# A third block's output projection split by branch, and the first weight steps of two seven-product stages reordered

## The chip, the cores and the metric

One core of one Trainium2 chip runs the whole program. The metric is device time in microseconds, the median of three runs; beside it stands one execution that was taken with the hardware profiler, and all rows below come from that one. The engines are PE (matmul), DVE (vector), ACT (activation), POOL (GpSimd) and SP, which here only issues DMAs. Each works through its own instructions strictly in the order in which the program emits them, so an instruction that waits holds up everything behind it on its engine.

## What is computed

Three transformer-like blocks run one after the other on an input of 1024 tokens by 1024 channels, in float32.

1. Block 1: retention and a spatial gate, an output projection, then a feed-forward layer of width 2816 with a short convolution.
2. Block 2: a convolution branch and a neighbourhood attention branch, then an output projection.
3. Block 3, which the change is mostly about:

```python
merged = concatenate([rms_norm(sb_out, sb_norm_g), rms_norm(swa_out, swa_norm_g)])
h = layer_norm(ALPHA * h + merged @ w_out)
h = layer_norm(ALPHA * h + (silu(gate) * up) @ w_down)     # gate, up = split(h @ w_gate_up)
```

`sb_out` is a stick-breaking attention over all earlier tokens (8 heads of 64), `swa_out` a softmax attention over a local window of 128 tokens (8 heads of 64). Rows 0 to 511 of `w_out` belong to the first, rows 512 to 1023 to the second, here called the SB part and the local part.

## The kernel before

**Data.** Activations lie transposed, channels on the 128 partitions, in two halves of 512 tokens. Every float32 matmul operand is split into a high part and a rest (`hhi`/`hlo` for activations, `whi`/`wlo` for weights), and a product takes three matmuls of 128x512: hi by hi, lo by hi, hi by lo. A weight tile is 128x1024; `w_load` (L369) takes its raw form from a DMA, rounds it on ACT (`whi`) and subtracts on POOL (`wlo`). Four such tiles exist at a time: `w_take` hands them out, `w_retire` loads the next ones.

**Order.** The order of emission is written by hand. A main generator issues big matmuls in sixes and yields a cost; `Driver` (L191) then runs background generators, up to 1.5 times that cost, each of which yields a cost and a delay. `force` emits all that is left of one generator on the spot. `Belt` (L235) is such a generator: it carries attention items, each in three steps (`sb1` scores, sigmoids, running product; `sb2` transposes; `sb3` times values), with a lag between the steps; `until(n)` emits items until n are done.

**Block 3's middle.** In a loop over four head pairs p (from L2258) the query and key projections (`qk`) run as main work, and the 24 items of the pair before run beside them. After the loop the 24 items of the last pair are left. From L2319 on the program emits the items one after the other up to the 80th of 96 with `fsb.until`, with no main work beside them, and between them two of the four `gen_mix` calls (L2289), which read the local branch back from DRAM (`yd`), scale it, transpose it (`yt`) and split it into the matmul operand. Then `out_abba` (L582) runs the whole output projection, 8 tiles of output channels by 2 halves by 8 chunks of input channels, with tiles `op` in PSUM: half 0 first, where the last 16 items run beside it, then half 1. It reloads four weight tiles for half 1, so it takes 12. After each half, `done` (L2376) starts the layer norm `gen_ln` (L651) of that half in the background: sums, mean, subtract, squares, row of factors, then 8 chunks, each scaled and split for the feed-forward's first matmuls (`fq`), which need them.

**Feed-forward.** `first_quad` (L548) runs the first matmuls, `fq`, over the two halves, and calls `hook(n)` (L1346) eight times, every 24 matmuls. In the hooks and behind them the six weight steps of the first seven-product group are emitted (`s_steps`, L1203): `s0` splits a quarter (`shi` on ACT, `slo` on POOL), `s1` makes two sums on POOL in place (`raw`), `s2` splits both, `s3` splits a whole tile (`whi`, `wlo`), `s4` makes two more sums, `s5` splits a second whole tile, which the next group's first product needs. `strassen` (L1256) then runs groups of seven products of 12 matmuls; in each it emits the six steps of the group after it. In a group `e1` is a copy of the first bank on ACT, `v1` adds the second bank to it on DVE, and the fourth product writes into that second bank, so it cannot start ahead of `v1`. Block 1 calls it with `lead=3` (a third pair of tiles runs as plain matmuls first), block 3 with `lead=2`.

Of the kernel before, what the change touches and what calls it, by code (L numbers as in the profile page):

```python
# [39 lines left out]
def _weights(a):  # L40
# [52 lines left out]
    t += abba(wa("w_out_3", 0, 1024))  # L93
# [5 lines left out]
S_TILES = ((38, 38), (178, 180))  # L99
# [199 lines left out]
class Kernel:  # L299
# [956 lines left out]
    def strassen(self, put, left, later, rest, tail):  # L1256
# [21 lines left out]
        for n in range(n_all):  # L1278
# [5 lines left out]
            if n + 1 < n_all:  # L1284
                steps = self.s_steps(n + 1, nxt)
                steps[0]()
                steps[1]()
            else:
                tail(0)
# [4 lines left out]
            if n == 0:  # L1294
                steps[2]()
                yield from prod(b2, cur["S24"], 0, T[2], True)
# [5 lines left out]
            if n == 0:  # L1302
                rest()
# [28 lines left out]
    def ffn(self, evac, put, later, add_last, done, by_half, alpha=None, lead=2):  # L1332
# [5 lines left out]
        with ExitStack() as ctx:  # L1338
# [7 lines left out]
            def hook(n):  # L1346
# [3 lines left out]
                elif n in (1, 2, 3):  # L1350
# [55 lines left out]
            if lead == 3:  # L1406
                ws = self.w_take(2)
                for f in steps:
                    f()
                self.s_dma(1)  # L1410
                for half in (1, 0):
                    for w in range(2):
                        ps = self.bank("fq")
                        yield from self.gemm_a(ps, ws[w], half)
                        put(2, w, half, ps, None)
                    if half:
# [553 lines left out]
    def block3(self):  # L1970
# [8 lines left out]
        roomy = []  # L1979

        def tmp(name):
            return self.h(name) if roomy else tp.tile([128, HF], F32, tag="t", name=name)
# [61 lines left out]
        def y_put(p, n, e, branch, ssq, write):  # L2044

            own = branch == 0 and p == 3
            if own:
                yc = Y[n][:, 384 + 64 * e:448 + 64 * e]
            else:
                if e == 0:  # L2050
                    YS[branch, p, n] = self.small(128, "ys")
                yc = YS[branch, p, n][:, 64 * e:64 * e + 64]
# [3 lines left out]
            if e == 1 and not own:  # L2056
# [200 lines left out]
        self.w_retire(2)  # L2257
        for p in range(4):  # L2258
            ws = self.w_take(2)
            for half in range(2):  # L2260
                for w in range(2):
# [25 lines left out]
        H2 = self.new_h()  # L2287

        def gen_mix(half, b):  # L2289

            n0 = 4 * half
            if not b:
                r = self.small(4, "r1")
                token_rms(r, ssb[:, n0:n0 + 4, :])
                ys = Y[n0:n0 + 4]
            else:
                r = rsw[:, n0:n0 + 4]
                ys = [self.h("yr") for _ in range(4)]
                for n in range(4):
                    nc.sync.dma_start(out=ys[n], in_=self.yd[n0 + n][:, 512:1024])  # L2300
                yield 0.0, 0.0
            for n in range(4):
                self.ts(ys[n], ys[n], r[:, n:n + 1])
            yield 0.0, 8470.0
            for c in range(4):
                ps = self.bank("yt")
# [160 lines left out]
```

## Time and profile before

| what | us |
|---|---|
| median of three runs | 3127.25 (3125.31 to 3131.94) |
| the profiled execution, device time | 3131.53 |
| its span, first to last instruction | 3129.7 |
| PE busy in the span | 2941.2 (94%) |
| DVE, POOL, ACT busy | 1803.3, 1432.9, 1284.8 |
| mean granted clock of PE | 0.964 of full |

The page's chain of work that ended last is made of PE lines for the largest part, and PE is busy in 94% of the span. So a saving must come from the few stretches in which PE stands still or runs at the lower clock. In the forty slices of the page these show as a digit below 9 in the rows PE and PEclk.

### The profile page before, as it was taken

Reading aid. Unit: us, or ns where it says so; the run is one execution under the profiler, and the core shown is the slowest. Engines: PE = TensorE matmul, PEld = TensorE weight load, DVE = VectorE, ACT = ScalarE, POOL = GpSimd, SP = SyncE. Lnnn points to the kernel's source line nnn. Section 1 sums busy time; section 2 is a strip of 40 time slices with the busy share of each in tenths; the row PEclk is TensorE's granted clock in tenths of the full one; section 3 lists DMA queues with packets and bytes.
Section 4 is the critical chain, followed back from the end, with each engine's and each line's share of the span. In section 5 each row is a group of like instructions: output and inputs, shape, how many; then the busy total and the mean of one; then the engine's idle time right before and its main releaser. Section 6 shows DMA issues by size and latency. Waiting matters only on the chain. (4 is left out here: it accounts for less than half of the span.)

```text
span 3129.7 us, 41397 instructions
## 1 busy us (share of the span) xinstructions
PE 2941.2 (94%) x15188; PEld 2499.6 (80%) x15188; DVE 1803.3 (58%) x3522; ACT 1284.8 (41%) x2493; POOL 1432.9 (46%) x1008
## 2 busy tenths in 40 slices
PE   8999998999999999889998989989899899999997
PEld 6898776888878877868897778977678688888886
DVE  6444246666665569966645665577667522224556
ACT  4232224444432153556673356654444422222223
POOL 4313434777743365862214342144333477774330
PEclk9999999999999999999998989999889999999998
DMA  4101241222252312131113232110222222225321
GB/s 159 33 23 51 72 134 41 81 81 81 81 188 82 108 49 80 40 109 50 44 39 118 84 121 64 42 32 27 68 68 98 84 81 81 86 79 179 108 81 54
DMA packets 114876, 248.96 MB, mean 80 GB/s; under 512 B 19696, under 2 KB 31600, under 8 KB 114672
## 3 DMA queue, kind: packets, MB, share of 16 engines
q1 hardware_dynamic: 114384, 246.01, 24.0%
q8 instruction: 120, 1.97, 0.3%
q14 instruction: 84, 0.69, 0.1%
q10 hardware_dynamic: 288, 0.30, 0.0%
HBM read 192.52 MB, written 53.74 MB: 79 GB/s over the span
## 5 line engine op out<-in xcount | busy, mean ns | idle before, releaser
L332 POOL TENSOR_TENSOR wlo<-raw,whi 128x1024 fp32r<-128x1024 f32 x240 | 582.2, 2436 | 862.0 <-ACT whi L326 846.5
L326 ACT ACTIVATE whi<-raw 128x1024 fp32r<-128x1024 f32 x240 | 248.3, 1053 | 537.0 <-PE dn L347 283.2
L332 DVE TENSOR_TENSOR X<-dn,X 128x512 f32<-128x512 f32 (+1 forms) x312 | 209.9, 676 | 161.7 <-PE dn L347 159.5
L347 PE MATMUL dn<-ghi,whi 128*128 128x512 f32 (+1 forms) x736 | 281.1, 382 | 0.6 <-DVE X L332 0.6
L347 PE MATMUL dn<-glo,whi 128*128 128x512 f32 (+1 forms) x736 | 280.2, 381 | 0.0
L347 PE MATMUL dn<-ghi,wlo 128*128 128x512 f32 (+1 forms) x736 | 280.2, 381 | 0.0
L332 POOL TENSOR_TENSOR raw<-raw 128x512 f32<-128x512 f32 x156 | 203.0, 1302 | 12.1
L332 POOL TENSOR_TENSOR slo<-raw,shi 128x512 fp32r<-128x512 f32 x117 | 150.7, 1302 | 106.2 <-ACT shi L326 104.9
L347 PE MATMUL p<-thi,shi 128*128 128x512 f32 x468 | 185.1, 395 | 13.9 <-DVE u L1105 9.8
L332 DVE TENSOR_TENSOR v<-p,e 128x512 f32<-128x512 f32 x78 | 53.8, 690 | 243.8 <-ACT e L326 194.3
L347 PE MATMUL p<-tlo,shi 128*128 128x512 f32 x468 | 183.9, 393 | 0.0
L347 PE MATMUL p<-hhi,wlo 128*128 128x512 f32 x468 | 182.2, 389 | 1.7 <-POOL wlo L332 1.7
L347 PE MATMUL p<-thi,slo 128*128 128x512 f32 x468 | 183.7, 393 | 0.0
L347 PE MATMUL p<-hhi,whi 128*128 128x512 f32 x468 | 182.1, 389 | 0.0
L347 PE MATMUL p<-hlo,whi 128*128 128x512 f32 x468 | 182.1, 389 | 0.0
L329 DVE SCALAR_TENSOR_TENSOR t<-u,vec,t 128x512 f32<-128x512 f32 x176 | 132.9, 755 | 79.5 <-ACT t L326 74.2
L347 PE MATMUL qk<-hhi,whi 128*128 128x512 f32 x384 | 162.2, 422 | 7.8 <-ACT hhi L326 7.2
L332 POOL TENSOR_TENSOR beta<-beta,f 128x511 f32<-128x511 f32 (+3 forms) x96 | 91.2, 956 | 154.0 <-DVE beta L336 137.8
L347 PEld LDWEIGHTS dn<-ghi,whi 128*128 128x128 f32 x736 | 139.2, 189 | 27.6 <-DVE X L332 1.3
L347 PEld LDWEIGHTS dn<-ghi,wlo 128*128 128x128 f32 x736 | 139.1, 189 | 26.4
L347 PEld LDWEIGHTS dn<-glo,whi 128*128 128x128 f32 x736 | 139.2, 189 | 26.0
L347 PE MATMUL op<-hhi,wlo 128*128 128x512 f32 x384 | 153.2, 399 | 4.0 <-POOL wlo L332 4.0
(400 smaller groups left out, 8150.7 us busy)
## 6 DMA issues: line engine op xcount, KB each, us to landing
raw<-in_wall SPq DMA_DIRECT2D x240, 512.0 KB, 3.8
gd<-g SPq DMA_DIRECT2D x88, 256.0 KB, 2.2
gx<-gd SPq DMA_DIRECT2D x88, 256.0 KB, 5.2
x2d<-X SPq DMA_DIRECT2D x64, 256.0 KB, 2.0
X<-x2d SPq DMA_DIRECT2D x64, 256.0 KB, 5.3
x<-in_xT SPq DMA_DIRECT2D x16, 256.0 KB, 6.0
X<-in_xT SPq DMA_DIRECT2D x16, 256.0 KB, 4.6
T<-in_rpbx SPq DMA_DIRECT2D x8, 448.0 KB, 3.6
```

The source lines that it names most:

```text
L326: self.nc.scalar.activation(out=out, in_=in_, func=func, bias=bias, scale=scale, **kw)
L329: self.nc.vector.scalar_tensor_tensor(out=out, in0=in0, scalar=s, in1=in1, op0=op0, op1=op1)
L332: (eng or self.nc.vector).tensor_tensor(out=out, in0=in0, in1=in1, op=op)
L347: self.nc.tensor.matmul(out=out, lhsT=lhsT, rhs=rhs, start=start, stop=stop, skip_group_check=more)
```

## The change

The third block's weight tiles of `w_out` are laid out by branch: four tiles for the local rows, then four for the SB rows, each with two output tiles side by side; 8 tiles are taken instead of 12. `out_abba` and the waits from L2319 on are gone. `gen_mix` moves ahead of the pair loop; the local mix of half 0 is put to the background in the last pair's second half, that of half 1 right after the loop. The local part of the projection (8 calls of `out_part`) then runs as main work with the last 24 items beside it, and writes ALPHA times the input plus its product back to X. The SB part follows, half 0 and half 1 with four calls each, and adds to X. So each X tile gets two additions from PSUM instead of one. The last head pair's attention output now goes to DRAM and back like that of the other pairs, and the items' temporaries keep their ten buffers to the end. In the feed-forward the steps `s0` to `s2` move: in block 1 from hooks 1, 2, 3 to hooks 3, 5, 7, with `s5` behind the first plain matmuls' evacuation; in the first group of both blocks, the next group's `s0` to `s2` move behind `e1` and `v1`.

```diff
--- before.py
+++ after.py
@@ -90,13 +90,15 @@
     q, k = wa("w_in_3", 0, 512), wa("w_in_3", 512, 1024)
     for p in range(4):
         t += [q[p], k[p]]
-    t += abba(wa("w_out_3", 0, 1024))
+    o = wa("w_out_3", 0, 1024)
+    for c in (slice(512, 1024), slice(0, 512)):
+        t += [np.concatenate([o[2 * i][:, c], o[2 * i + 1][:, c]], axis=1) for i in range(4)]
     t += ffn("w_gate_up_3", "w_down_3")
     return np.stack(t)
 
 
 
-S_TILES = ((38, 38), (178, 180))
+S_TILES = ((38, 38), (174, 176))
 
 _VEC = [
     ("mix_norm_g", 8), ("ret_norm_g", 4), ("ffn_norm_g", 8), ("conv_b", 44), ("final_norm_g", 8),
@@ -1283,8 +1285,9 @@
                 self.s_dma(n + 2)
             if n + 1 < n_all:
                 steps = self.s_steps(n + 1, nxt)
-                steps[0]()
-                steps[1]()
+                if n > 0:
+                    steps[0]()
+                    steps[1]()
             else:
                 tail(0)
             if n > 0:
@@ -1292,7 +1295,6 @@
                 steps[2]()
             yield from prod(b1, cur["A1"], 0, B11, True)
             if n == 0:
-                steps[2]()
                 yield from prod(b2, cur["S24"], 0, T[2], True)
             if n + 1 == n_all:
                 tail(1)
@@ -1300,6 +1302,8 @@
             self.act(e1, b1, AF.Copy)
             self.tt(v1, b2, e1, ALU.add)
             if n == 0:
+                for f in steps[0:3]:
+                    f()
                 rest()
             steps[3]()
             for f in left[0]:
@@ -1347,7 +1351,7 @@
 
                 if n == 0 and lead == 3:
                     self.s_dma(0)
-                elif n in (1, 2, 3):
+                elif n in ((1, 2, 3) if lead == 2 else (3, 5, 7)):
                     steps.pop(0)()
                 elif n in (4, 6):
                     next(gt)
@@ -1405,14 +1409,16 @@
             left = ([], [], [])
             if lead == 3:
                 ws = self.w_take(2)
-                for f in steps:
-                    f()
+                steps.pop(0)()
+                steps.pop(0)()
                 self.s_dma(1)
                 for half in (1, 0):
                     for w in range(2):
                         ps = self.bank("fq")
                         yield from self.gemm_a(ps, ws[w], half)
                         put(2, w, half, ps, None)
+                        if steps:
+                            steps.pop(0)()
                     if half:
                         next(gt)
                         next(gt)
@@ -1976,10 +1982,9 @@
         po2 = ctx.enter_context(tc.tile_pool(name="b3p", bufs=2, space=PSUM))
         ctx1 = ExitStack()
         kp = ctx1.enter_context(tc.tile_pool(name="b3k", bufs=4))
-        roomy = []
 
         def tmp(name):
-            return self.h(name) if roomy else tp.tile([128, HF], F32, tag="t", name=name)
+            return tp.tile([128, HF], F32, tag="t", name=name)
 
         identb = pp.tile([128, 128], mybir.dt.bfloat16, tag="ib", bufs=1, name="identb")
         sbmb = pp.tile([128, 128], mybir.dt.bfloat16, tag="mb", bufs=1, name="sbmb")
@@ -2043,17 +2048,13 @@
 
         def y_put(p, n, e, branch, ssq, write):
 
-            own = branch == 0 and p == 3
-            if own:
-                yc = Y[n][:, 384 + 64 * e:448 + 64 * e]
-            else:
-                if e == 0:
-                    YS[branch, p, n] = self.small(128, "ys")
-                yc = YS[branch, p, n][:, 64 * e:64 * e + 64]
+            if e == 0:
+                YS[branch, p, n] = self.small(128, "ys")
+            yc = YS[branch, p, n][:, 64 * e:64 * e + 64]
             write(yc)
             sq = self.small(64, "ysq")
             self.act(sq, yc, AF.Square, accum=ssq[:, n, 2 * p + e:2 * p + e + 1])
-            if e == 1 and not own:
+            if e == 1:
                 nc.sync.dma_start(out=self.yd[n][:, 512 * branch + 128 * p:512 * branch + 128 * p + 128],
                                   in_=YS.pop((branch, p, n)))
 
@@ -2255,9 +2256,39 @@
         fsw.put(*[sw_unit(p, n) for p in range(4) for n in range(4, 8)])
         yield from values(ws, 1, range(3, 8))
         self.w_retire(2)
+        H2 = self.new_h()
+
+        def gen_mix(half, b):
+
+            n0 = 4 * half
+            ys = [self.h("yr") for _ in range(4)]
+            for n in range(4):
+                nc.sync.dma_start(out=ys[n], in_=self.yd[n0 + n][:, 512 * b:512 * b + 512])
+            r = rsw[:, n0:n0 + 4]
+            if not b:
+                r = self.small(4, "r1")
+                token_rms(r, ssb[:, n0:n0 + 4, :])
+            yield 0.0, 4000.0
+            for n in range(4):
+                self.ts(ys[n], ys[n], r[:, n:n + 1])
+            yield 0.0, 2500.0
+            for c in range(4):
+                ps = self.bank("yt")
+                for n in range(4):
+                    nc.tensor.transpose(ps[:, 128 * n:128 * n + 128], ys[n][:, 128 * c:128 * c + 128], self.ident)
+                hi, lo = self.h("hhi", F32R), self.h("hlo", F32R)
+                H2[0][c + 4 * b][half], H2[1][c + 4 * b][half] = hi, lo
+                g = self.v("swa_norm_g_3" if b else "sb_norm_g_3", c)
+                self.act(hi, ps, AF.Identity, scale=g)
+                self.stt(lo, ps, g, hi, ALU.mult, ALU.subtract)
+                yield 450.0, 200.0
+
+        sws, sbs = [None, None], [None, None]
         for p in range(4):
             ws = self.w_take(2)
             for half in range(2):
+                if p == 3 and half == 1:
+                    sws[0] = drv.add(gen_mix(0, 1))
                 for w in range(2):
                     ps = self.bank("qk")
                     yield from self.gemm_a(ps, ws[w], half)
@@ -2284,54 +2315,6 @@
                 fsb.put(*[u[i, e][0] for i in (3, 0, 2, 1) for e in range(2)])
                 fsb.put(*[u[i, e][x] for i in (7, 6, 5, 4) for x in range(2) for e in range(2)])
 
-        H2 = self.new_h()
-
-        def gen_mix(half, b):
...
-                ys = Y[n0:n0 + 4]
-            else:
...
-                for n in range(4):
-                    nc.sync.dma_start(out=ys[n], in_=self.yd[n0 + n][:, 512:1024])
-                yield 0.0, 0.0
-            for n in range(4):
-                self.ts(ys[n], ys[n], r[:, n:n + 1])
-            yield 0.0, 8470.0
...
-        roomy.append(True)
-        fsb.lag = 6
-        sws = [gen_mix(0, 1), gen_mix(1, 1)]
-        next(sws[0])
-        next(sws[1])
-        fsb.until(70)
-        next(sws[0])
-        fsb.until(72)
-        Y = [self.h("yr") for _ in range(8)]
-        for n in range(8):
-            nc.sync.dma_start(out=Y[n][:, 0:384], in_=self.yd[n][:, 0:384])
-        drv.force(sws[0])
-        next(sws[1])
-        fsb.until(76)
-        drv.force(sws[1])
-        fsb.until(80)
-        sbs = [drv.add(gen_mix(0, 0)), None]
-        self.H = H2
         X = [[None, None] for _ in range(8)]
         self.X = X
         acc, seen = [None, None], [[], []]
@@ -2351,11 +2334,6 @@
             elif n > 2:
                 self.tt(acc[half], acc[half], X[j][half][:, sl], ALU.add)
 
-        def o_evac(j, half, ps):
-            x = X[j][half]
-            self.stt(x, x, ALPHA, ps, ALU.mult, ALU.add)
-            acc_x(j, half)
-
         def ln1_sink(half):
             def sink(j, x, b):
                 hi, lo = self.h("hhi", F32R), self.h("hlo", F32R)
@@ -2379,15 +2357,56 @@
             acc[half] = None
             seen[half] = []
 
-        def middle():
-
-            fsb.finish()
-            ctx1.close()
-            ctx.close()
-            sbs[1] = drv.add(gen_mix(1, 0))
-
-        yield from self.out_abba(o_load, o_evac, done, (4, 5, 6, 7, 0, 1, 2, 3), lambda half: None,
-                                 lambda half: drv.force(sbs[half]), middle)
+
+        def out_part(w, t, half, b):
+            pss = [self.bank("op") for _ in range(2)]
+            whi, wlo = w
+            for k in range(4):
+                hi, lo = H2[0][4 * b + k][half], H2[1][4 * b + k][half]
+                for i, ps in enumerate(pss):
+                    c = slice(512 * i + 128 * k, 512 * i + 128 * k + 128)
+                    self.mm(ps, whi[:, c], hi, k == 0, False)
+                    self.mm(ps, whi[:, c], lo, False, False)
+                    self.mm(ps, wlo[:, c], hi, False, k == 3)
+                yield 6 * 216.0
+            for i, ps in enumerate(pss):
+                x = X[2 * t + i][half]
+                if b:
+                    self.stt(x, x, ALPHA, ps, ALU.mult, ALU.add)
+                else:
+                    self.tt(x, ps, x, ALU.add)
+                    acc_x(2 * t + i, half)
+
+        sws[1] = drv.add(gen_mix(1, 1))
+        drv.force(sws[0])
+        for t in (0, 2):
+            ws = self.w_take(2)
+            for half in range(2):
+                for j in range(2 * t, 2 * t + 4):
+                    o_load(j, half)
+            for half in range(2):
+                if half and not t:
+                    drv.force(sws[1])
+                if half and t:
+                    fsb.until(80)
+                    sbs[0] = drv.add(gen_mix(0, 0))
+                for i in range(2):
+                    yield from out_part(ws[i], t + i, half, 1)
+                    if half:
+                        self.w_retire(1)
+        ws = self.w_take(4)
+        for half in range(2):
+            drv.force(sbs[half])
+            for t in range(4):
+                if half == 0 and t == 2:
+                    fsb.finish()
+                    ctx1.close()
+                    ctx.close()
+                    sbs[1] = drv.add(gen_mix(1, 0))
+                yield from out_part(ws[t], t, half, 0)
+                if half:
+                    self.w_retire(1)
+            done(half)
         self.H, self.hs, self.rs = H3, new_hs, None
 
         A = {}
```

## Rows read from the trace of the kernel before

**Rows 1.** Busy time by stretch: stretch, length, then each engine's us, PEclk, DMA share, GB/s

```profile
2170.60:2239.00 68.40, 62.17 (x388) 51.35 (x388) 47.99 (x105) 33.93 (x96) 30.23 (x30) 0.97 0.09 24
2236.40:2288.20 51.80, 38.14 (x188) 33.31 (x189) 35.42 (x76) 24.11 (x67) 19.65 (x17) 0.62 0.36 117
2288.20:2337.50 49.30, 47.56 (x294) 40.92 (x294) 31.95 (x73) 20.58 (x50) 18.89 (x14) 0.98 0.23 72
2337.50:2407.00 69.50, 69.50 (x332) 58.17 (x331) 46.51 (x70) 25.76 (x38) 17.80 (x8) 1.00 0.29 95
2500.00:2600.00 100.00, 100.00 (x441) 82.14 (x440) 24.88 (x37) 28.65 (x42) 70.61 (x47) 1.00 0.23 79
```

**Rows 2.** PE's groups from 2236.4 to 2288.2: count, busy us, mean ns, idle before

```profile
L347 PE MATMUL sbo<-v,pt 128*128 128x64 f32 x76 | 16.0, 367 | 12.5 <-DVE pt L2173 10.0 <-DVE yr L2186 2.5
...
L347 PE MATMUL sb<-ks,qq 128*128 128x512 f32 (+3 forms) x14 | 7.6, 544 | 0.0
L2308 PE MATMUL yt<-ident,yr 128*128 128x128 f32 x32 | 6.8, 404 | 0.0
```

**Rows 3.** Timeline, DVE around the two layer norms: start, us, instruction, idle before

```profile
2360.00 0.69 DVE L329 SCALAR_TENSOR_TENSOR X<-X,op 128x512 f32<-128x512 f32 x1 [4.03 <-PE op L347]
...
2384.11 1.40 DVE L329 SCALAR_TENSOR_TENSOR X<-X,vec,row 128x512 f32<-128x512 f32 x2 [2.89 <-PE row L455]
2385.65 0.75 DVE L329 SCALAR_TENSOR_TENSOR hlo<-X,vec,hhi 128x512 fp32r<-128x512 f32 x1
...
2411.75 0.16 DVE L336 TENSOR_SCALAR mean<-ln 128x4 f32<-128x4 f32 x1 [1.15 <-PE ln L347]
...
2428.23 1.41 DVE L329 SCALAR_TENSOR_TENSOR X<-X,vec,row 128x512 f32<-128x512 f32 x2 [1.92 <-PE row L455]
```

**Rows 4.** DMA issues of the whole run: tiles, count, KB each, us to landing

```profile
X<-x2d SPq DMA_DIRECT2D x64, 256.0 KB, 5.3
...
yd<-ys SPq DMA_DIRECT2D x56, 64.0 KB, 1.6
...
yr<-yd SPq DMA_DIRECT2D x8, 256.0 KB, 5.3
```

**Rows 5.** Timeline, block 1's feed-forward, first matmuls

```profile
456.14 0.16 DVE L336 TENSOR_SCALAR ms<-st 128x4 f32<-128x4 f32 x1 [1.07 <-PE st L347]
...
459.31 0.63 PE L347 MATMUL fq<-hlo,whi 128*128 128x512 f32 x1
459.73 0.63 PE L347 MATMUL fq<-hhi,wlo 128*128 128x512 f32 x1
463.56 0.63 ACT L326 ACTIVATE shi<-raw 128x512 fp32r<-128x512 f32 x1 [10.09 <-DMA raw<-in_wall]
464.10 0.19 ACT L326 ACTIVATE rs_s<-ms 128x4 f32<-128x4 f32 x1
...
466.29 1.09 PE L455 MATMUL row<-ident,r 128*128 128x128 f32 x4 [5.93 <-DVE r L332]
```

**Rows 6.** Timeline, block 1's first group of seven products

```profile
537.75 0.63 ACT L326 ACTIVATE shi<-raw 128x512 fp32r<-128x512 f32 x1
...
542.97 0.58 ACT L326 ACTIVATE e<-p 128x512 f32<-128x512 f32 x1
...
544.32 0.79 PE L347 MATMUL p<-thi,shi 128*128 128x512 f32 x1 [8.37 <-DVE u L1105]
...
551.28 2.40 POOL L332 TENSOR_TENSOR wlo<-raw,whi 128x1024 fp32r<-128x1024 f32 x1 [1.38 <-ACT whi L326]
...
558.13 0.39 PE L347 MATMUL p<-thi,wlo 128*128 128x512 f32 x1
```

**Rows 7.** Timeline, block 3's first group of seven products

```profile
2472.82 0.58 ACT L326 ACTIVATE e<-p 128x512 f32<-128x512 f32 x1
...
2474.18 0.55 PE L347 MATMUL p<-thi,shi 128*128 128x512 f32 x1 [2.62 <-DVE v L332]
...
2488.88 0.50 PE L347 MATMUL p<-thi,wlo 128*128 128x512 f32 x1 [1.47 <-POOL wlo L332]
```

More of the change, by code (lines that the diff above doesn't have):

```diff
@@ L2285, in block3 @@
                 fsb.put(*[u[i, e][x] for i in (7, 6, 5, 4) for x in range(2) for e in range(2)])
-        H2 = self.new_h()
-        def gen_mix(half, b):
[L2291 to L2294, printed above, removed]
-                ys = Y[n0:n0 + 4]
-            else:
-                r = rsw[:, n0:n0 + 4]
-                ys = [self.h("yr") for _ in range(4)]
-                for n in range(4):
-                    nc.sync.dma_start(out=ys[n], in_=self.yd[n0 + n][:, 512:1024])
-                yield 0.0, 0.0
-            for n in range(4):
-                self.ts(ys[n], ys[n], r[:, n:n + 1])
-            yield 0.0, 8470.0
-            for c in range(4):
-                ps = self.bank("yt")
-                for n in range(4):
-                    nc.tensor.transpose(ps[:, 128 * n:128 * n + 128], ys[n][:, 128 * c:128 * c + 128], self.ident)
-                hi, lo = self.h("hhi", F32R), self.h("hlo", F32R)
-                H2[0][c + 4 * b][half], H2[1][c + 4 * b][half] = hi, lo
-                g = self.v("swa_norm_g_3" if b else "sb_norm_g_3", c)
-                self.act(hi, ps, AF.Identity, scale=g)
-                self.stt(lo, ps, g, hi, ALU.mult, ALU.subtract)
-                yield 450.0, 200.0
-        roomy.append(True)
-        fsb.lag = 6
-        sws = [gen_mix(0, 1), gen_mix(1, 1)]
-        next(sws[0])
-        next(sws[1])
-        fsb.until(70)
-        next(sws[0])
-        fsb.until(72)
-        Y = [self.h("yr") for _ in range(8)]
-        for n in range(8):
-            nc.sync.dma_start(out=Y[n][:, 0:384], in_=self.yd[n][:, 0:384])
-        drv.force(sws[0])
-        next(sws[1])
-        fsb.until(76)
-        drv.force(sws[1])
-        fsb.until(80)
-        sbs = [drv.add(gen_mix(0, 0)), None]
-        self.H = H2
         X = [[None, None] for _ in range(8)]
```

## The prediction, made before the changed kernel had run

> **What bounds the kernel now.** I read the page's busy table first: PE 2941 of 3129.7 us. So the question is where PE does not run at full rate, and the forty slices show few such places; the change touches three. I then took the busy time by stretch around the third block's attention end [rows 1]. The reader should compare the second stretch with its neighbours. It is 51.8 us long, PE is busy 38.1 of them, and the granted clock is 0.62: this is where the program emits attention items with no main matmuls beside them. Its groups [rows 2] show PE waiting 12.5 us for DVE's copies, one item's chain running at its own latency. The clock makes the rest dear: in a stretch at full clock (2.4 GHz) 441 matmuls fill 100 us, 0.227 us each [rows 1], while two neighbours at the lower level (1.2 GHz) start 0.42 us apart [rows 5]. The other two places are short stalls at the start of the two feed-forward layers [rows 5 to 7].
>
> **Part 1, the local projection beside the last items.** First, what the 51.8 us hold as work. The stage ahead of them had 96 qk matmuls and 24 items in 62.2 us of busy PE [rows 1]; 96 x 0.227 = 21.8, so an item costs 40.4 / 24 = 1.68 us of PE. The stretch has 14 items and 32 transposes [rows 2]: 14 x 1.68 + 4 (6.8 us at 0.62 clock) = 27.5 us. If matmuls of the projection fill everything else, 51.8 - 27.5 = **24.3 us** go. That is the ceiling, for the 384 matmuls of the projection stay 384 and are only moved.
>
> From it comes off what the mixture loses. The stage with qk kept PE busy in 62.17 of 68.4 us (9% lost), the next stretch with items in 47.56 of 49.3 (3.5%) [rows 1]. On the 67 us of work that now run mixed (24 items and some 27 us of projection) that is 2.4 to 6 us. DVE gets 16 more evacuations of 0.69 us [rows 3], 11 us, nine or ten of them beside items where it was already busy 70% (47.99 of 68.4) [rows 1]; so I go near the upper end, and less the 1.7 us that the old stretch lost anyway: **-4** (-1 to -7).
>
> The local mixes are moved ahead: their loads on SP, scaling on DVE and transposes on PE lie beside qk or local matmuls, and count in the sum above. Two things are new waits. The first evacuation on DVE needs its X tile, whose load now stands on SP behind weight loads and lands in 5.3 us [rows 4]; the scans of the items are queued behind that evacuation. PE has two banks of other work, so 0 to 4 us. And the last pair's output goes through DRAM: store 1.6 us and load 5.3 us [rows 4], then scaling and a first transpose, some 10 us, against two calls of `out_part` as cover, 48 x 0.227 = 10.9 us: 0 to 4 us again. Together **-1** (0 to -8), near nothing because each cover is about as long as its wait. The Trainium skill bears on that round trip: "DMA: Bandwidth & Descriptors", section "Anatomy of one DMA", fits a transfer as about 2.0 us plus its bytes over 436 GB/s, stated for the GpSimd path; as an estimate from that page, store and load take 2.2 + 2.6 = 4.8 us, against 6.9 by the rows, so the cover would be long enough by either and the sum would be 1 us better by the page. I keep the rows.
>
> The other removals cost or give nothing: four weight tiles less to load, round and subtract, all of it work of ACT, POOL and DMA beside a busy PE. If that cover were gone they would return about a weight's latency, and they don't.
>
> **Part 2, what is late next: the layer norm.** Before, half 1's whole projection (192 matmuls, 43.7 us) stood behind half 0's layer norm. After, only the SB half does: 96 x 0.227 = 21.8 us, with 16 transposes and the norm's own small matmuls about 26. From half 0's last evacuation to the first finished chunk the norm took 2360.0 to 2386.4, 26.4 us [rows 3]: just covered. But its eight chunks follow at two DVE instructions of 0.74 each (1.48 us) [rows 3] against 6 x 0.227 = 1.36 us of matmuls per chunk, and the same window has to take half 1's eight evacuations and eight additions, which used to have twice the time (11 us of DVE), and the SB mix of half 1. The leftover chunks are forced out ahead of `fq`, so half 1's norm finds its first DVE instruction (the mean [rows 3]) queued behind them. PE then stands at that norm's row transposes, and later at half 1's first chunk: from mean to first scaled chunk the norm needs 2411.75 to 2428.23, 16.5 us [rows 3]. Adding up from half 0's last matmul: 26 to the first chunk + 12 for the eight + 4 until the row is through + 16 to half 1's first chunk (its `fq` partner runs below that) + 12 + 11 for the second pair of tiles = 81 to 84 us until the last `fq`, where 26 + 43.7 + 4 = 74 would be free of waits and before had 2 us of waits. So **-9** (0 if DVE keeps up, -14 if the clock falls too).
>
> Part 1 and 2: 24.3 - 4 - 1 - 9 = 10.3 us.
>
> **Part 3, block 1's hooks.** In `fq` of half 0, ACT stood 10.09 us for the DMA that brings `s0`'s raw tile, and behind it in ACT's order the square root `rs_s` of half 1's norm, whose input `ms` was there at 456.3, ran at 464.1; PE stood 5.93 us at the row transposes [rows 5]. `s0` moves from hook 1 to hook 3, 48 matmuls later and behind `rs_s` in ACT's order. Then `r` is ready by 457.8, ahead of the row's turn at 460.2, and nothing stalls: 5.93, and up to 1.8 more if the nine `fq` behind the row, by my reading still at the lower pitch of 0.42, run at 0.227. Against that, half 1's chunks follow the row by the same DVE chain, which moves by less than PE does. **+7** (5 to 8). `s1` and `s2` move past half 1's chunks on POOL and ACT, where they delayed them by 1.1 us before; `s2` now delays one ACT evacuation by that. `s5` moved behind one evacuation takes ACT's wait for POOL's sums from in front of it: nothing on PE.
>
> **Part 4, the first groups.** In block 1, `e1` stood in ACT's order behind `s0` and `s2`, whose `shi` wait for POOL: 537.75 to 542.97, and PE waited 8.37 us (the row names a small DVE write, the one behind `v1`) and started at the lower clock [rows 6]. After, `e1` comes at 537.8, PE goes on at about 539.1: 5.2 us earlier, and 12 matmuls up to 2.4 us faster. But POOL's chain does not move: `s0` now starts 0.6 us later, and its end is `s5`'s `wlo`, 553.7 in the rows, so 554.3. The next group's third matmul, at 558.13, needs it [rows 6]. So PE waits there, and only 558.1 - 554.3, less 0.5, **+3.3** stay (0 to 8). In block 3 the same: PE's 2.62 us go, with the lower clock 4.4 us; before, the next group already waited 1.47 us for `wlo` at 2488.88 [rows 7], which moves only by the reordering of the T splits, **+1.6** (0 to 4.5).
>
> **Sum.** 10.3 + 7 + 3.3 + 1.6 = 22.2 us. The profiled execution took 3131.5, so 3109.3 for a like one; the median of the runs lies 4.3 below that: 3127.25 - 22.2 = **3105.0 us**.
>
> **Rivals.**
> - *POOL does not hold the first groups, or the norm is hidden.* If `wlo` keeps up, part 4 gives 7.6 + 4.4 instead of 4.9; if DVE keeps up, part 2's 9 us stay. For it: DVE is busy 46.5 of 69.5 us in the old half 1 [rows 1]. Against: the order on both engines is fixed. Some 8 us more: 3097, with both 3089.
> - *The stall in block 1 only moves.* `s0`'s wait for the DMA then stands ahead of half 1's chunks on ACT. For: the tile lands at 463.5, about when hook 3 comes. Against: the chunks' first splits are emitted ahead of it. Part 3 then gives 2: 3110.
> - *The change does not do what it says.* If the local operands come late (the mixes need free tiles while qk's operands are held) or the items are spent in the first half of the local part and the rest of it runs alone, the items' chain still sets the pace and part 1 gives 9 or less; with part 2 at -9, blocks 1 and 3 alone are left: 3127 - 12 = 3115, or 3124 if the row transposes stall too.
> - *Slower: PSUM banks.* `out_part` holds two of six banks from its first matmul to its DVE evacuation, where most of the old calls held one; items need up to three. If PE has to wait for a bank at each of the 16 calls, the price is the DVE queue's delay, some 3 us (two scans of 1.3 and an evacuation), 48 us in all: 3127 - 22 + 48 = 3153. It decides from (22 + 6) / 16 = 1.8 us per call. Against it: in the old mixture DVE waited for PE's `op` (4.03 us before an evacuation [rows 3]) and not the other way.
>
> **How the numbers follow.** Forecast as summed, 0.52; the better rival 0.23; the stall that moves 0.08; not doing what it says 0.11; banks 0.06. The range takes the terms' bounds and the better and the poorer rival, without their extremes: 3089 to 3118. A change within 0.2% (6.3 us) is about what a measurement of this kernel cannot tell from none. Faster by more means below 3121: 0.52 + 0.23 + 0.08 and half of 0.11, 0.88; same 0.07; slower 0.05.
>
> **What would show it.** Part 1: no stretch with a clock near 0.6 after the last qk matmul, and the end of half 0's projection near 2360 less block 1's gain, with half of half 1 done. Part 2: PE idle at `row` and at `fq` with DVE as the releaser. Part 3: `rs_s` ahead of `shi` on ACT, no idle at `row` near 460. Part 4: `e` right behind the evacuations, PE's wait moved to `wlo` one group later. It would be wrong if `op` matmuls waited for DVE throughout, or if half 1's chunks in block 1 stalled PE by as much as the row did.

## The result and the profile after

The changed kernel takes **3145.15 us** (median of 6 runs, 3141.17 to 3152.89); the kernel before took 3128.22 us beside it (6 runs, 3125.31 to 3133.53). The ratio is **1.0053, 95% interval 1.0037 to 1.0069**: 17 us slower, where 22 us less were forecast, and outside the range of 3089 to 3118. The profiled execution of the changed kernel took 3141.59 us, 10.1 more than the one of before (3131.53).

First the page's busy line of the kernel after. Then busy time by stretch (stretch, length, PE, PEld, DVE, ACT, POOL, PEclk, DMA share, GB/s): one row of the kernel before, then five of the kernel after. The last four stretches answer to those of [rows 1], cut at the last `qk` and the last `op` matmul of the kernel after (in [rows 1] the second stretch starts 2.3 us behind the last `qk`).

```profile
PE 2946.8 (94%) x15188; PEld 2493.0 (79%) x15188; DVE 1814.4 (58%) x3538; ACT 1277.8 (41%) x2487; POOL 1423.1 (45%) x1004
```

```profile
600.00:700.00 100.00, 100.00 (x443) 82.83 (x442) 62.61 (x110) 46.14 (x68) 70.66 (x46) 1.00 0.27 90
```

```profile
600.00:700.00 100.00, 100.00 (x436) 81.80 (x435) 63.65 (x111) 45.92 (x68) 70.92 (x47) 1.00 0.24 79
2161.30:2236.70 75.40, 64.93 (x384) 54.47 (x383) 52.29 (x112) 35.54 (x97) 29.84 (x31) 0.91 0.12 36
2236.70:2288.50 51.80, 38.24 (x209) 30.10 (x208) 28.49 (x60) 18.49 (x54) 16.94 (x15) 0.84 0.26 88
2288.50:2337.80 49.30, 48.01 (x273) 40.82 (x273) 31.29 (x69) 16.99 (x48) 16.43 (x16) 0.97 0.26 85
2337.80:2405.40 67.60, 64.25 (x335) 53.07 (x334) 47.60 (x82) 16.67 (x31) 15.42 (x7) 1.00 0.18 55
```

Three things stand here. The stretch behind the last `qk` matmul has PE idle for 13.6 of 51.8 us, as before (13.7), at a better clock (0.84 against 0.62). The last `qk` stage has grown to 75.4 us. And block 1's feed-forward layer, far from the projection, now does 436 matmuls in 100 us at a granted clock of 1.00, where it did 443 before at the same clock (first row).

The next table is worked out from the starts of the matmuls in each trace, in us. "Groups" runs from the last `fq` to the last `p` matmul of block 1, "last qk" over the 96 `qk` matmuls of the last stage, "op" from the last `qk` to the last `op`, "norm" from there to the last `fq` of block 3. The lower kernels are the experiments.

```
                           fq blk1  groups  down blk1  last qk     op   norm
before                       80.0    379.0     240.3     67.4   172.7   48.2
after                        71.4    384.5     243.9     75.4   168.8   58.8
e1_steps_only                71.4    383.0     244.1     67.4   172.4   48.2
e2_split_only                78.8    379.1     240.9     73.0   171.1   59.3
e3_loads_early               71.4    385.8     243.4     74.1   157.7   58.8
e4_loads_early_scale_pool    71.4    385.9     243.7     75.6   170.7   61.7
e5_steps_aligned             71.4    381.2     240.6     67.4   172.6   48.4
e6_gap128                    79.8    383.3     244.8     68.4   171.8   48.4
e7_split_early_aligned       71.4    379.6     240.5     75.3   158.8   58.9
e8_no_sums                   71.4    381.0     240.4     74.8   157.9   56.3
e9_norm_sooner               71.4    379.6     240.6     74.1   163.4   61.2
e10_first_mix_late           71.4    379.6     240.2     67.4   166.7   59.1
e11_hooks_aligned            71.4    379.9     240.6     67.4   172.4   48.3
e12_low_on_pool              71.4    380.9     240.3     73.0   158.1   54.1
```

After less before: -8.6, +5.5, +3.6, +8.0, -3.9, +10.6, together +15.2. Block 2's own projection, which no edit touches, took 262.2 us before and 256.2 after (from its last `qk` to its last `op`; 256 to 264 over all fourteen kernels), so this pair of profiles shows some 6 us less than the medians do. This stretch scatters from profile to profile; why was not looked into.

Where PE stood in the op stage: timeline of after, SP's issues, DVE and PE (start, us, instruction, idle time before it and what ended it).

```profile
2244.98 3.59 SPq L364 DMA_DIRECT2D raw<-in_wall  x2
2248.66 4.17 SPq L2325 DMA_DIRECT2D X<-x2d  x8
2252.92 4.28 SPq L2266 DMA_DIRECT2D yr<-yd  x4
...
2249.32 0.68 DVE L2174 COPY pt<-sbt 128x512 f32<-128x512 f32 x1
2260.43 0.49 DVE L338 TENSOR_SCALAR yr<-yr,rsw 128x512 f32<-128x512 f32 x1 [10.44 <-DMA yr<-yd]
...
2253.11 0.40 PE L349 MATMUL op<-hhi,wlo 128*128 128x512 f32 x1
2261.07 1.05 PE L2278 MATMUL yt<-ident,yr 128*128 128x128 f32 x2 [7.57 <-DVE yr L338]
```

The local mix of half 1 is forced after two calls of `out_part`. Its four loads stand on SP behind two weight tiles and eight X tiles, 3 MB, and land at 2260. DVE works in order, so the items' scans (their running products) behind the first scaling stand for the same 10.4 us, and what ACT and PE have to do for those items waits behind them: PE stands 7.57 us.

### The profile page after: what moved, and what is told of

It is laid out like the page before. It is cut to its first block, busy times and chain, and to the rows that moved or that the text cites. A ratio compares the mean times of both kernels' runs of the same rounds, so it can differ in the third digit from the quotient of the medians.

```text
span 3139.8 us, 41383 instructions
## 1 busy us (share of the span) xinstructions
PE 2946.8 (94%) x15188; PEld 2493.0 (79%) x15188; DVE 1814.4 (58%) x3538; ACT 1277.8 (41%) x2487; POOL 1423.1 (45%) x1004
## 5 line engine op out<-in xcount | busy, mean ns | idle before, releaser
L334 POOL TENSOR_TENSOR wlo<-raw,whi 128x1024 fp32r<-128x1024 f32 x236 | 570.8, 2427 | 896.8 <-ACT whi L328 856.1
```

Source lines behind the costliest of these rows:

```text
L334: (eng or self.nc.vector).tensor_tensor(out=out, in0=in0, in1=in1, op=op)
```

## The experiments

**e1_steps_only and e2_split_only: each half of the change alone.** Below, "pitch" is the time from the start of one matmul to the start of the next. The diff of e1 is that of the hooks, of the steps around the first `fq` pair and of the first group; that of e2 is the rest.

> The kernel before with only the reordered weight steps of the feed-forward layers (the two hook edits and the edit of the first group), the output projection as before. Theory: the hooks are worth the 8.6 us that block 1's last fq came earlier in the changed kernel, and the 9 us that its Strassen groups and down-projection then lost (0.230 us from one matmul to the next, 0.227 before) are not made by these steps; then 3128 - 8 = 3120 us, with fq's end 7 to 9 us earlier and the pitch at 0.227. Rival: the steps themselves slow the groups; then the pitch is 0.230 again from about 540 us on, and the time is 3127 to 3130.

> The kernel before with only the third block's output projection split by branch. Theory: the split loses 4 us up to its last matmul (8 in the last qk stage, some 11 at the local mix of half 1, against what it saves) and 8 more in the layer norm behind it; 3128 + 12 = 3140 us. Rival: the slower pitch of block 1 comes with the split (other weight tiles, other buffers), and the split costs all of the 17 us and the 9 that the hooks gained: 3149 to 3154, with a pitch of 0.230 in block 1.

e1: ratio 1.0001 (0.9990 to 1.0011). `fq` is 8.6 us shorter, and the groups and the down-projection lose 7.8 of it at the pitch of 0.230. So the first theory fell: the slower pitch comes with the steps. e2: 1.0053 (1.0040 to 1.0066), some 17 us and more than the 12 expected, with the pitch at 0.227, which its rival had at 0.230. The split alone costs as much as the whole change; the steps' gain and their loss had cancelled.

**e5_steps_aligned and e6_gap128: why the steps slow matmuls that they don't touch.** A tile pool keeps one set of buffers for each tag. In the kernel before, hook 1 takes the first tile of the tag `e` before an evacuation takes the first of the tag `u`. With `s0` at hook 3 the order is turned round, and the pool places tags in order of first use. Four `u` tiles of 2080 bytes then lie below the `e` tiles of block 1: 8320 bytes, which is 4 x 2048 + 128. e5 is e1 with one unused tile of the tag `e` taken first; e6 is the kernel before with an unused tile of 128 bytes ahead of the tag `e`.

```
e5: self.up = ctx.enter_context(self.tc.tile_pool(name="ffn", bufs=4))
   +self.up.tile([128, 512], F32R, tag="e", bufs=12, name="e0")
e6: (same place, kernel before)
   +if lead == 3:
   +    self.up.tile([128, 1024], F32, tag="raw", bufs=2, name="r0")
   +    self.up.tile([128, 32], F32, tag="gap", bufs=1, name="gap")
```

> As e1_steps_only, with one empty tile of the tag e taken when the feed-forward pool is opened, so that the tiles of that tag (shi, slo, and every second group's ghi, glo) lie as in the kernel before. In e1 the tag u was first used ahead of the tag e, since s0 had moved behind the first evacuations, and so the e tiles of block 1 lie 8320 bytes higher in each partition, which is 128 bytes more than a multiple of their size of 2048. Theory: the pitch of 0.230 us comes from this shift; with it gone the pitch is 0.227, and the hooks' 8 us stay to the end: ratio 0.997 to 0.998 to the kernel before (6 to 9 us less). Rival: the pitch comes from the order of the work; then 0.230 again and a ratio of 1.000.

> The kernel before, every instruction as it was, with an unused tile of 128 bytes a partition taken ahead of the e tiles of block 1's feed-forward layer. Theory: the shift by 128 bytes alone makes the pitch 0.230 instead of 0.227 from about 540 to 1190 us; 8 to 10 us more, ratio 1.0026 to 1.0032. Rival: it was not the shift but where else the tiles came to lie (8320 bytes higher, u below them), or the order of the work; then the time of the kernel before, ratio 1.000.

e5: 0.9978 (0.9967 to 0.9989), 7 us less than before. e6: 1.0020 (1.0012 to 1.0029), 6 us more (8 to 10 were expected), with every instruction as it was. In e6 the groups and the down-projection take 383.3 and 244.8 us, as in after; in e5 381.2 and 240.6. Groups of PE instructions between 600 and 880 us, first of e6, then of e5 (count, busy us, mean ns of one, idle before):

```profile
L347 PE MATMUL p<-thi,shi 128*128 128x512 f32 x177 | 70.1, 396 | 0.0
L347 PE MATMUL p<-tlo,shi 128*128 128x512 f32 x176 | 69.5, 395 | 0.0
...
L347 PE MATMUL p<-hhi,whi 128*128 128x512 f32 x174 | 68.0, 391 | 0.0
...
L347 PE MATMUL p<-tlo,whi 128*128 128x512 f32 x56 | 21.8, 389 | 0.0
L347 PE MATMUL p<-thi,whi 128*128 128x512 f32 x56 | 21.8, 389 | 0.0
```

```profile
L347 PE MATMUL p<-tlo,shi 128*128 128x512 f32 x177 | 68.9, 389 | 0.0
L347 PE MATMUL p<-thi,slo 128*128 128x512 f32 x177 | 68.9, 389 | 0.0
```

The matmuls with a shifted operand are slower: `shi` and `slo` against `thi` or `tlo`, not `whi` against `thi`. By starts, the former are 0.233 us apart in e6 and in after, 0.227 in before and e5. The `hhi` products, which have no shifted tile, lose a little (0.229 for `hhi` with `whi`), but only in the last matmul ahead of a shifted product and the first three to seven behind one. The down-projection confirms it: of e6's groups of 96 matmuls every second one has its `ghi` and `glo` in `e` tiles, and those are 0.2333 us apart, the ones between 0.2268. So the shift of 128 bytes is the cause. In before, all operand tiles of these matmuls start 288 bytes past a multiple of 2048; in e6 and in after, those of block 1's tag `e` start 416 past one. Whether the difference to the other operand's tile matters or the place by itself can't be told, for no matmul had both of its tiles shifted. Other offsets were not tried, and why it costs stays open.

**e3_loads_early: the 10.4 us on DVE.**

```
 (in the qk loop, ahead of w_retire)
+if p == 3:
+    sws[1] = gen_mix(1, 1)
+    next(sws[1])
+    drv.add(sws[1], 4000.0)
 ...
-sws[1] = drv.add(gen_mix(1, 1))
```

> The changed kernel, with the four loads of the local mix's second half issued ahead of the next weight loads and the eight X loads instead of behind them. Theory: DVE's 10.4 us stand at the first scaled yr goes to under 2, PE's 7.6 us at its transpose go, and with the lower clock behind it 8 to 11 us are saved: 3135 to 3137. Rival: the stand only moves, to the X tile of the first evacuation or to the weights, whose loads now come later by the 3 us of these four: 3141 to 3145.

Ratio 1.0014 (1.0006 to 1.0023) against 1.0053 for the change: 12 us back, nearly all in the op stage (168.8 to 157.7). DVE waits for no `yr` there any more, and no wait of PE between 2240 and 2290 us is longer than 1.6 us; the first rows of e3's waits (engine, tile, releaser: us in total, times, longest):

```profile
PE sb L349 <- DVE ks L334: 1.6, 1, 1.6
PE sbt L2172 <- issue: 1.3, 2, 1.1
PE sbo L349 <- DVE pt L2174: 1.3, 2, 0.9
```

**e4_loads_early_scale_pool: the scalings on POOL.** `self.ts(ys[n], ys[n], r[:, n:n + 1], eng=nc.gpsimd)`.

> As e3_loads_early, and the sixteen scalings of the mixes' tiles (0.48 us each) on POOL instead of DVE. Theory: in the last qk stage DVE's chain of scans sets the pace, and the mix put there costs it 4.7 us, of which the scalings are 1.9; taking them off DVE saves 2 to 4 us in that stage and up to 2 us before the layer norm: 3131 to 3134. Rival: POOL is slower at it and delays the transposes, or the weights behind them: no gain over e3_loads_early, or 1 to 4 us of loss.

1.0072 (1.0060 to 1.0085), some 18 us more than e3. The theory fell, and the rival has the sign but only 1 to 4 us: a scaling takes 1.6 us on POOL, PE waits 9.7 us for them in the op stage (waits of e4 from 2236 us on), and the last `qk` stage gains nothing.

```profile
PE yt L2278 <- POOL yr L338: 9.7, 9, 1.2
```

**e7_split_early_aligned: both repairs together.** The edits of e3 and e5 on the changed kernel.

> The changed kernel with both repairs: the loads of the local mix's second half early, as in e3_loads_early, and the e tiles as in the kernel before. Theory: the two add up; e3's ratio of 1.0014 less the pitch's 9 us (0.0029) gives 0.9985, 3 to 6 us below the kernel before. Rival: the pitch is no matter of the tiles; 1.0014 again.

0.9996 (0.9987 to 1.0006), 18 us less than the changed kernel. The tiles bring 6 us on top of e3, as much as e6 costs, and not the 9 of the theory, so the fully repaired change is not to be told from the kernel before. The experiments that follow start from here.

**e10_first_mix_late: the last qk stage.**

```
 if p == 3 and half == 1:
-    sws[0] = drv.add(gen_mix(0, 1))
+    sws[0] = gen_mix(0, 1)
+    next(sws[0])
```

> As e7_split_early_aligned, with the scaling and transposes of half 0's local mix put behind the last qk matmul instead of beside the last qk half (their loads stay where they are). Theory: the last qk stage, 245 to 247 us from its first matmul against 236 to 239 in kernels without the split, loses 8 us because the mix's 4.7 us of DVE delay the scans and the clock falls; without it that stage is back at 236 to 239, and the stage behind it, 158 to 159 us, pays 4 to 6 for a mix that nothing covers: 2 to 4 us less than e7. Rival: the qk stage's 8 us have another cause (the weight loads, the h buffers that the loads take): it stays at 245, and e7's time grows by 4 to 6 us.

1.0002 (0.9993 to 1.0011). The stage is back at 67.4 us, as without the split, so the mix is what lengthens it; but the op stage takes 166.7 instead of 158.8 us. The theory is right that the mix is the cause and wrong on the saving: the mix costs 8 us at either place. Busy time in the last `qk` stage of e7 and of e10, PE's longest wait in that stage of after (e7 has the same), and its longest behind that stage in e10:

```profile
2163.40:2238.70 75.30, 64.78 (x383) 54.31 (x382) 52.29 (x112) 35.48 (x97) 29.79 (x31) 0.91 0.12 36
```

```profile
2159.80:2227.20 67.40, 60.78 (x377) 50.14 (x375) 47.81 (x104) 32.92 (x94) 30.01 (x31) 0.97 0.14 40
```

```profile
PE sbt L2172 <- ACT beta L328: 3.8, 2, 3.4
```

```profile
PE yt L2279 <- DVE yr L338: 9.6, 3, 5.6
```

In e7's stage DVE has 4.5 us more to do and ACT 2.6. PE stands 3.9 us longer and is busy 4.0 us more, with the 16 transposes of the mix and a clock of 0.91 where e10 has 0.97. Which of these sets the pace was not separated: PE's longest wait there is for ACT, and e4, which took the scalings off DVE, did not shorten the stage, though POOL's slower scalings may hide a gain.

**e8_no_sums, e9_norm_sooner and e12_low_on_pool: what holds the layer norm.** In after PE stands between 2400 and 2465 us for:

```profile
PE ln L349 <- DVE acc L334: 4.5, 1, 4.5
PE fq L349 <- ACT hhi L328: 2.0, 1, 2.0
PE row L457 <- DVE mean L338: 1.6, 1, 1.6
```

Parts of the three edits (the experiments change e7):

```
e8:  -elif n > 2:
     -    self.tt(acc[half], acc[half], X[j][half][:, sl], ALU.add)
e9:  -slack=100.0 if half else 1800.0), 2000.0)
     +slack=100.0), 2000.0 if half else 600.0)
e12: (half 0's low(), instead of the one stt on DVE; the act was in rest())
     +self.act(x, x, AF.Identity, bias=b)
     +self.tt(lo, x, hi, ALU.subtract, nc.gpsimd)
```

> As e7_split_early_aligned, with the sums over X for the layer norm's mean left out from the third tile on (12 of 14 additions on DVE, 0.69 to 2.7 us each), so its mean is of two tiles only. Theory: DVE is what holds the layer norm of half 0 behind half 1's short SB part; without the additions PE's 4.5 us wait at the sum, its 1.6 us at the mean and most of the rest go, 6 to 9 us less than e7. Rival: the norm is held by its own chain (ACT's and PE's steps in turn); then 0 to 3 us less, and PE waits at the row transposes or for hhi instead.

> As e7_split_early_aligned, with the due times of half 0's layer norm in block 3 shortened (first step 600 instead of 2000 ns behind the half, 100 instead of 1800 ns added at two of its steps). Theory: these times were set for a norm with 43.7 us of matmuls behind it; with 22 us they leave the row transposes too late, DVE stood 4.6 us for the row in e8, and the norm's first chunk comes 4 to 5 us earlier: 3 to 5 us less than e7, ratio 0.998. Rival: DVE has no more room (12.3 us busy of 13 ahead of the row in e7), its queue only changes order, and the time stays within 1 us of e7.

> As e7_split_early_aligned, with the eight low halves of half 0's normed chunks (0.75 us each on DVE, behind 0.74 for the scaling) made on POOL from a chunk to which ACT has added the bias. Theory: after half 0's sums are done the bound is DVE's 12 us for these chunks, in whose order half 1's last additions and its mean stand; six of them go, PE's 4.5 us at the sum and 1.6 us at the mean shrink to under 2 together, and the stretch from op's end to fq's end falls from 58.9 to 53 to 55 us: 4 to 6 less than e7, ratio 0.998. Rival: POOL takes 1.3 us for each and holds DVE's own additions up meanwhile, so fq waits for hlo instead: 58 us or more, ratio 1.000 or above.

e8 leaves out most of the sums, so its mean is not the right one: 0.9950 (0.9937 to 0.9963), 14 us less than e7. Its profile is 20.6 us shorter than e7's, but only 2.6 of these lie in the norm's stretch and 0.9 in the op stage; 7 lie in block 2's projection, which scatters, some 4 in block 3's feed-forward layer, the others in small pieces elsewhere, all of it unexplained. By the stretch its rival holds, and the sums alone are not what holds the norm: PE's wait moved to the mean, queued behind half 0's chunks (first row below). e9: 1.0021 (1.0012 to 1.0029), 8 us more than e7; theory and rival fell. With the norm emitted sooner, half 0's chunks stand ahead of half 1's evacuations and sums on DVE, and PE waits 11.0 us for those (second row). e12: **0.9971 (0.9959 to 0.9983)**, its norm stretch 54.1 us, as expected: with eight instructions off DVE the waits for `acc` and for `mean` are gone, and the longest that are left are the last two rows. Waits of PE, e8 from 2380, e9 from 2385, e12 from 2394 us:

```profile
PE row L457 <- DVE mean L338: 6.4, 1, 6.4
```

```profile
PE ln L349 <- DVE acc L334: 11.0, 1, 11.0
```

```profile
PE fq L349 <- ACT hhi L328: 2.1, 1, 2.1
PE fq L349 <- POOL hlo L334: 1.6, 1, 1.6
```

e12 beats both kernels, 9 us under the one before; e5, which leaves the projection as it was, is 7 us under it, and the intervals overlap. The last three columns of the table add up to 285.2 us in e12, and to 288.0 to 288.6 in the five kernels without the split. So the split, with all the repairs that were tried, is worth some 3 us in these stretches.

**e11_hooks_aligned: the first group's order.** As e5, without the edit of the first group.

> As e5_steps_aligned, but the first seven-product group's order as in the kernel before: only the hooks and the steps around the first fq pair are changed. Theory: the reordered first group is worth nothing (in block 1 the Strassen stage took 379.4 to 381.0 us with it and 378.8 without): the time is that of e5 within 2 us, ratio 0.997 to 0.998, and the stage is at 379 again. Rival: the first group's order does carry 3 us as predicted: ratio 0.9985 to 0.999.

0.9984 (0.9975 to 0.9993), not to be told from e5; the time alone lies between theory and rival. The stretch decides: the groups take 379.9 us in e11, 379.0 and 379.1 in before and e2, and 379.6 to 381.2 in the kernels that have the new order and the old tile places. The reordered first group is worth nothing.

## Why the prediction was wrong, and where it was right

**What bounds the kernel** was read rightly as far as PE goes, but the moved local mixes were costed as PE work alone. What they need of DVE, ACT and the DMA queue had no term.

**Part 1, -19.3 forecast, +4.1 measured** (last qk +8.0, op -3.9). One sentence failed twice, and one term was too small. The sentence is that the loads, scalings and transposes of the local mixes "lie beside qk or local matmuls, and count in the sum above". First, it passed over the loads of half 1's mix, because SP's order past the weight and X loads was followed for X alone; the wait stood there, at `yr`, and e3 measures it at 11 to 12 us. The two new waits that the text did price at -1 were there and cost PE about as little as it said: from 2290 us to the last `op` DVE stands 9.1 us for X tiles and 5.2 us for `yr`, and PE 1.9 us at what these hold up, of 4.4 us that it stands there in all. Waits of DVE, then of PE, in after from 2290 to 2405 us:

```profile
DVE X L331 <- DMA X<-x2d: 9.1, 4, 6.2
...
DVE yr L338 <- DMA yr<-yd: 5.2, 5, 2.6
...
PE yt L2278 <- DVE yr L338: 0.9, 1, 0.9
...
PE yt L2278 <- DVE X L334: 0.7, 1, 0.7
...
PE sbt L2172 <- DVE X L331: 0.3, 1, 0.3
```

Second, the scaling and the transposes of half 0's mix beside `qk` were to cost nothing beyond their PE time; they lengthen the last `qk` stage by 8 us, and cost as much when they are moved behind it (e10). The term that was too small is that for the mixture, -4 (-1 to -7): with the loads repaired the op stage is 13.9 to 15.0 us shorter than before (e7, e3), where the sum had 19.3, and PE still stands 11.1 of e3's 157.7 us there; which of the remaining waits makes the difference stays open. In all, part 1 with the loads repaired gains 6 to 9 us (last qk and op: 240.1 before, 234.1 in e7, 231.8 in e3, 231.1 in e12).

**Part 2, -9 forecast, -10.6 measured.** The mechanism was right: DVE's queue, the mean behind half 0's chunks, PE standing at `row` and at `fq`, and at the sum, which the text had not named. From half 0's last `op` matmul to the last `fq` it took 85.1 us, where the text added up 81 to 84. The -9 itself does not follow from that sum: 81 to 84, less 74 and the 2 us of waits before, is 5 to 8, so that it came so near is in part luck. e12, which takes work off DVE, gets 4.7 of the 10.6 us back (54.1 against e7's 58.9); what the other 6 are was not tested.

**Part 3, +7 (5 to 8) forecast, +8.6 measured.** The mechanism was right. `rs_s` now runs at 457.51 on ACT, before `shi`, where it had run at 464.1 [rows 5], and the row's transposes start at 461.30 without a wait.

```profile
457.51 0.20 ACT L328 ACTIVATE rs_s<-ms 128x4 f32<-128x4 f32 x1 [2.87 <-DVE ms L338]
...
461.30 0.88 PE L457 MATMUL row<-ident,r 128*128 128x128 f32 x4
```

**What had no term at all** is that moving `s0` turned round the order in which two tags are first used, and so moved the tiles: 9 us lost in after by groups and down-projection (5.5 + 3.6), of which the tiles make 8.3 by the same stretches of after and e7. The step reads "`s0` moves from hook 1 to hook 3, 48 matmuls later", and counts time and order only.

**Part 4, +3.3 and +1.6 forecast, nothing measured.** In block 1 `e` did come earlier, and the 8.37 us wait [rows 6] became 2.56 us. But the next wait is not at `wlo` one group later; it is in the same group, 3.85 us at the second evacuation. Timeline of after:

```profile
532.76 0.50 PE L349 MATMUL p<-thi,shi 128*128 128x512 f32 x1 [2.56 <-DVE u L1107]
...
535.25 0.63 ACT L328 ACTIVATE shi<-raw 128x512 fp32r<-128x512 f32 x1 [2.76 <-POOL raw L334]
...
538.09 0.77 ACT L328 ACTIVATE t<-u,vec 128x512 f32<-128x512 f32 x1
...
538.89 1.55 DVE L331 SCALAR_TENSOR_TENSOR t<-u,vec,t 128x512 f32<-128x512 f32 x2 [5.00 <-ACT t L328]
...
543.23 0.68 DVE L334 TENSOR_TENSOR v<-p,e 128x512 f32<-128x512 f32 x1
...
543.96 0.80 PE L349 MATMUL p<-thi,shi 128*128 128x512 f32 x1 [3.85 <-DVE v L334]
```

The failed step is that only `s5`'s `wlo` would hold the next products. The `shi` that wait for POOL, moved behind `e`, now stand ahead of the convolution's `t` on ACT; DVE waits for `t`, and the evacuation is queued behind it on DVE. So POOL's chain still holds PE, by another road than the forecast's. Block 3's 1.6 us didn't come either: its groups take 396.0 us after 396.4.

**The rivals.** Banks: PE stood 1.0 us behind evacuations of `X` (the last two of the rows above), where 16 calls at 1.8 us were needed to decide. It is the only rival that had the change slower (3153), and its cause is not what was found. That the change doesn't do what it says was nearest for part 1 (local operands late), but was priced as a lost gain and not as a stop of DVE for every item. No rival saw the tiles.

## What to carry to other kernels

When work moves to another queue position, list every transfer it needs and what then stands ahead of each on its queue; the one that isn't listed is the one that stops an in-order engine, and with it all that shares the engine. Work put beside a stage can cost far more than its PE time, by what it takes of the other engines that the stage needs. And reordering the first uses of buffers can move them: compare tile addresses before blaming the order of instructions, and take the tags' first tiles in a fixed order, as e5 does.

## What the runs showed of the hardware

A matmul whose two operand tiles started 128 bytes apart, counted modulo 2048, was followed by the next after 0.233 us on the mean instead of 0.227, some 2.7% more, in all five kernels that had such tiles (after, e1, e3, e4, e6); the granted clock was 1.00 with and without. The Trainium skill, "SBUF — State Buffer", section "SBUF: two separate sides", says that PE never waits on anyone on the engine side of SBUF; the page speaks there of engines that share ports. These runs show that the place of a tile can still cost PE time, but not by what mechanism.

DVE's additions of two SBUF tiles took 0.69 us, or, where they started inside a subtraction of POOL, until that was done. Timeline of after, in the layer norm:

```profile
2396.42 2.42 POOL L334 TENSOR_TENSOR wlo<-raw,whi 128x1024 fp32r<-128x1024 f32 x1 [1.13 <-ACT whi L328]
...
2397.27 2.12 DVE L334 TENSOR_TENSOR acc<-acc,X 128x512 f32<-128x512 f32 x1
...
2400.03 0.69 DVE L334 TENSOR_TENSOR acc<-acc,X 128x512 f32<-128x512 f32 x1
...
2402.13 2.40 POOL L334 TENSOR_TENSOR wlo<-raw,whi 128x1024 fp32r<-128x1024 f32 x1 [3.29 <-ACT whi L328]
...
2402.74 2.34 DVE L334 TENSOR_TENSOR acc<-acc,X 128x512 f32<-128x512 f32 x1
```

Both long ones end 0.55 us after POOL's (2399.39 after 2398.84, 2405.08 after 2404.53). The same page and section describe this: the two engines share a port pair as a lock held for the whole instruction. The trace agrees. It makes some DVE work of a tight stretch three times as dear: the forecast took 0.69 us for each addition, though the kernel before already had additions of 2.2 to 2.8 us there.
